# Condition maps of both layers as whole fp32 products on four quarters of the matrix array's columns

## The chip, the cores and the metric

The kernel runs on one core of one Trainium2 chip. The metric is the device time of one execution in microseconds (us), taken as the median of several runs; lower is better.

## The reference, cut to what matters

The reference is two layers of a hybrid trunk (windowed attention beside a state-space scan, then multi-head latent attention) on 1024 latent tokens and 128 context tokens of width 1024. Each layer begins with a norm that is shifted and scaled, and ends with a residual that is gated, and these three vectors come from a linear map of a condition vector. Latent and context tokens have one condition each:

```python
def modulation(cond, w_ada, b_ada):          # w_ada (1024, 3072) per layer, b_ada (3072,)
    m = jax.nn.silu(cond) @ w_ada + b_ada
    shift, scale, gate = jnp.split(m[:, None, :], 3, axis=-1)
    return shift, scale, gate

h = rms_norm(x, norm_w[layer]) * (1.0 + scale) + shift      # at the start of each layer
x = x + gate * out                                          # at its end
```

So each layer has a map of 2 rows by 1024 by 3072. It is small in arithmetic (two rows), but its weights are 12 MB per layer.

## The kernel before

**The condition maps.** `condition()` makes silu of both condition vectors with the contraction dimension on the partitions: `cond32[128, 8, 2]` in fp32, and `condT[128, 8, 4]`, which holds the rounded part and the remainder of both in float32r. `modulation(sp, l, j, parts)` then makes 256 of the 3072 columns of layer `l`, so there are 12 calls per layer and 24 in all. Columns j = 0..3 are the shift, 4..7 the scale, 8..11 the gate. Each call loads a bias row of 1 KB (L348) and four weight blocks of 128 x 2 x 256 (256 KB each, L301 in `raw_block`), and it has two forms:

- `parts` true (19 calls): `slab` splits each block into a rounded part (cast on ACT, L249) and a remainder (subtraction on DVE, L250). PE multiplies each of 8 contraction blocks with both parts: 16 float32r products with 4 stationary and 256 moving columns (L355, L356). The rows of `acc` are then latent and context of the rounded and of the remainder part of the condition.
- `parts` false (5 calls, all in the first stage): 8 fp32 products with 2 stationary columns, straight from the loaded block (L361). The trace has two records for each fp32 product, called passes here.

ACT copies `acc` to `rows` (L362), whose last row is the bias. A last product with the constant `sel` adds the rows of each condition and the bias: for shift and scale two fp32 products that also turn the columns to the partitions (L368), for the gate one (L376). DVE writes `shift` or `scl` (L371, L373); for the gate, ACT copies to `gs` (L378) and a DMA stores it in `gate_d`.

**Where the calls stand.** Eight calls (shift and scale of layer 0) are in the first stage, among the transposes of the normalised input (`hidden0`, L439) that need their results. The other sixteen are in the list `later`: one call of `some_modulation` makes the next one. Twelve are made in `convs` (the convolutions of layer 0, beside `attention0`), four in `gates1` (the gate projection of layer 1).

**What sets the order.** The code is built with a scheduler that places each engine's instructions by its own timing; only marked instructions stay in program order. All DMAs of loads and stores are issued by the SP engine, in its order, and a DMA whose destination is still in use holds up those behind it. Loaded weight blocks go through the ring `wr` of 8 buffers in fp32 (3 when the ring is reopened after the first stage), which the condition maps share with all split weights. `acc` and `pt` come from a PSUM ring of two, tag `tr`. `rows` has 2 buffers, `gs` one.

Of the kernel before, what the change touches and what calls it, by code (L numbers as in the profile page):

```python
# [15 lines left out]
ALU = mybir.AluOpType  # L16
# [38 lines left out]
def shape_constants():  # L55
    i = np.arange(128)
    ident = np.eye(128, dtype=np.float32)
    upper = (i[:, None] <= i[None, :]).astype(np.float32)
    lower = (i[:, None] >= i[None, :]).astype(np.float32)
    after = (i[:, None] > i[None, :]).astype(np.float32)  # L60
    before = (i[:, None] < i[None, :]).astype(np.float32)
    tri = np.stack([upper, lower, after, before, np.ones((128, 128), np.float32)], axis=1)
    c0, s0 = rope_tables(64)
    c1, s1 = rope_tables(32)
    rope0 = np.stack([c0, s0], axis=1)
    rope1 = np.stack([c1, s1], axis=1)
    rope1t = np.ascontiguousarray(np.stack([np.tile(c1.T, (4, 1)), np.tile(s1.T, (4, 1))], axis=1))
    sel = np.zeros((5, 2), np.float32)
    sel[[0, 2, 4], 0] = 1.0
    sel[[1, 3, 4], 1] = 1.0  # L70
    prev_ok = i[:, None] <= i[None, :]
    next_ok = i[:, None] >= i[None, :]
    mq = np.zeros((128, 640), np.float32)
    mq[:, 128:256] = np.where(prev_ok, 0.0, NEG)
    mq[:, 384:512] = np.where(next_ok, 0.0, NEG)
    mk = np.stack([np.where(prev_ok.T, 0.0, NEG), np.where(next_ok.T, 0.0, NEG)], axis=1).astype(np.float32)
    return {"k_ident": ident, "k_tri": tri, "k_rope0": rope0, "k_rope1": rope1, "k_rope1t": rope1t,
            "k_sel": sel, "k_mq": mq, "k_mk": mk}
# [142 lines left out]
def hybrid_trunk(ctx: ExitStack, tc: tile.TileContext, I, O, dbg=None, stage=99):  # L221
# [37 lines left out]


    ident = const("ident", [128, 128], I["k_ident"])
    sels = {n: const(f"sel{n}", [n + 1, 2], I["k_sel"][4 - n:5]) for n in (2, 4)}
    vecs = cp.tile([128, 96], F32, tag="vecs", name="vecs")
    shift = cp.tile([128, 2, KT, 2], F32, tag="shift", name="shift")
    scl = cp.tile([128, 2, KT, 2], F32, tag="scl", name="scl")
    cond32 = cp.tile([128, KT, 2], F32, tag="cond32", name="cond32")
    condT = cp.tile([128, KT, 4], F32R, tag="condT", name="condT")
    dts = cp.tile([128, NT, 32], F32, tag="dts", name="dts")
    normw = vecs[:, 0:16].rearrange("p (l k) -> p l k", l=2)

# [46 lines left out]
    def condition():  # L317
        with Space(mem) as p:
# [5 lines left out]
            dve.scalar_tensor_tensor(th, th, 1.0, cin, ALU.add, ALU.mult)  # L324
            pt = psum("tr", "pt")
            pe.transpose(pt[:, 0:16], th, ident[0:16, 0:16])
            full = cond32
            dve.tensor_scalar(full, pt[:, 0:16].rearrange("p (j k) -> p k j", j=2), 0.5, None, ALU.mult)
            split(condT[:, :, 0:2], condT[:, :, 2:4], full)
# [10 lines left out]
            dve.tensor_copy(vecs, pt[:, 0:96])  # L340
            dve.tensor_scalar(vecs[:, 16:76], vecs[:, 16:76], 0.5, None, ALU.mult)

    def modulation(sp, l, j, parts):

        c0 = j * 256
        n = 4 if parts else 2
        rows = cp.tile([5, 256], F32, tag="rows", name="rows", bufs=2)[0:n + 1]
        dma.dma_start(rows[n:n + 1], I["ada_b"][l:l + 1, c0:c0 + 256])  # L348
        acc = psum("tr", "acc")
        v = I["ada_w"][l].rearrange("(k p) n -> p k n", p=128)  # L350
        if parts:
            for k in range(KT):
                if k % 2 == 0:
                    wh, wl = slab(I["ada_w"][l], c0, rows=(k, k + 2), sp=sp, bufs=2)
                pe.matmul(acc[0:4, 0:256], condT[:, k], wh[:, k % 2], start=(k == 0), stop=False)  # L355
                pe.matmul(acc[0:4, 0:256], condT[:, k], wl[:, k % 2], start=False, stop=(k == KT - 1))  # L356
        else:
            for k in range(KT):
                if k % 2 == 0:
                    raw = raw_block([128, 2, 256], v[:, k:k + 2, c0:c0 + 256])  # L360
                pe.matmul(acc[0:2, 0:256], cond32[:, k], raw[:, k % 2], start=(k == 0), stop=(k == KT - 1))  # L361
        act.copy(rows[0:n], acc[0:n, 0:256])  # L362
        sel = sels[n]
        cg, ks = j // 4, slice((j % 4) * 2, (j % 4) * 2 + 2)
        if cg < 2:
            pt = psum("tr", "pt")
            for k in range(2):
                pe.matmul(pt[:, 2 * k:2 * k + 2], rows[:, k * 128:(k + 1) * 128], sel, start=True, stop=True)  # L368
            pv = pt[:, 0:4].rearrange("p (k j) -> p k j", j=2)
            if cg == 0:  # L370
                dve.tensor_copy(shift[:, l, ks], pv)  # L371
            else:
                dve.scalar_tensor_tensor(scl[:, l, ks], pv, 1.0, normw[:, l, ks].unsqueeze(2).broadcast_to([128, 2, 2]), ALU.add, ALU.mult)  # L373
        else:
            pt = psum("tr", "pt")
            pe.matmul(pt[0:2, 0:256], sel, rows, start=True, stop=True)  # L376
            gs = cp.tile([2, 256], F32, tag="gs", name="gs", bufs=1)
# [5 lines left out]
    def some_modulation(sp, n=1):  # L383
        for _ in range(n):
            if later:
                modulation(sp, *later.pop(0), True)

    def rstd_of(p, ssq, n, width):

# [52 lines left out]
            modulate(0, cond, k, hT[c][0][:, k, a:b], hT[c][1][:, k, a:b], pt[:, a:b], tmp[:, 0:b - a])  # L442
    for t in range(3):
        normalised(t)
    p1.reserve("wh", 512, 5, "R")
    p1.reserve("wl", 512, 5, "R")
    for j in range(4):
        modulation(p1, 0, j, False)
        modulation(p1, 0, 4 + j, j > 0)
        if j == 0:  # L450
            for t in range(3, 6):
                normalised(t)
        for c in range(2):
            for k in (2 * j, 2 * j + 1):
                hidden0(c, k)
# [391 lines left out]
    def convs(p):  # L847
# [18 lines left out]
        for n, sb in enumerate(order):  # L866
            for b in range(2):
# [19 lines left out]
                if fb < 9:  # L887
# [9 lines left out]
                some_modulation(p, 2 if b and n < 2 else 1)  # L897
                yield
        yield from beside
    p4, p = Space(mem), Space(mem)  # L900
# [3 lines left out]
    with Space(mem, right=True) as pa:  # L904
        cv = convs(p)
        at = attention0(pa)
        p.reserve("wh", 512, 2, "R")
        p.reserve("wl", 512, 2, "R")
# [318 lines left out]
    def gates1(p):  # L1227
# [8 lines left out]
        for n, (i, c) in enumerate(units):  # L1236
            if n % NCH == 0:
                weights(n // NCH + 2)
            dma.dma_start(g1_d[i, :, c * CH:(c + 1) * CH], silu_of(p, fm_proj(ws[i], 0, h1T, c)))
            if n < 8 and n % 2:  # L1240
                some_modulation(p)
            if n == 8:
                p.drop("wh", "wl")
            if i == 7:
                h1p.drop(f"h10{c}", f"h11{c}")
            yield
# [449 lines left out]
```

## Time and profile before

| | before |
|---|---|
| median of 3 runs | 1850.03 us |
| lowest and highest | 1843.2 and 1850.26 us |
| profiled execution, its own time | 1849.66 us |
| its span, first to last instruction | 1847.8 us |
| PE matmul busy | 1713.8 us (93% of the span) |
| PE weight load busy | 1315.1 us (71%) |
| DVE, ACT, POOL busy | 1045.4, 817.2, 744.2 us |
| mean granted TensorE clock | 0.958 |

PE is the matrix engine (PEld its weight loads), DVE, ACT and POOL the vector, scalar and general engines, SP the engine that issues the DMAs. A row of the profile names the line of the kernel, the engine, what is written and read, and the shapes: `128*4 128x256` is a product with 128 contraction rows and 4 stationary columns, 256 moving columns. Matmuls are pipelined, so the pace of a row of products is the distance from start to start, and not the duration of one.

### The profile page before, as it was taken

How to read it: one execution, taken by the hardware profiler on the slowest of the kernel's cores; microseconds unless marked ns; L12 is line 12 of the kernel's file. 1: busy time of each engine (PE TensorE's matmuls, PEld its weight loads, DVE VectorE, ACT ScalarE, POOL GpSimd, SP SyncE). 2: the span in 40 equal slices, each digit the busy share in tenths (PEclk: the TensorE clock that was granted, in tenths of full speed). 3: DMA queues.
4: the chain of work that ended last, by engine and by line, in shares of the span. 5: the costliest groups of instructions: out<-in, count | busy, mean ns of one | idle time of the engine just before them, and what ended most of it. 6: DMA issues, size and time to landing. Idle time of an engine off the chain costs nothing.

```text
span 1847.8 us, 27078 instructions
## 1 busy us (share of the span) xinstructions
PE 1713.8 (93%) x9031; PEld 1315.1 (71%) x9031; DVE 1045.4 (57%) x1989; ACT 817.2 (44%) x1873; POOL 744.2 (40%) x741
## 2 busy tenths in 40 slices
PE   6899999999998878998899999999999998998898
PEld 3799999877775766666688898655665665654486
DVE  4665545655546467777665434655665664564243
ACT  4532323665655354444444322444545544545321
POOL 3510000133343345665623010466666665565432
PEclk9999999999999888999999999899999998999899
DMA  7423423434435697565463532020120121104342
GB/s 260 125 81 93 121 62 111 131 101 132 115 105 146 195 284 240 166 208 159 167 180 85 165 110 79 11 61 23 52 71 23 45 75 28 37 29 122 109 154 91
DMA packets 210655, 210.26 MB, mean 114 GB/s; under 512 B 36162, under 2 KB 175504, under 8 KB 210516
## 3 DMA queue, kind: packets, MB, share of 16 engines
q1 hardware_dynamic: 210372, 208.40, 37.8%
q8 instruction: 72, 1.18, 0.3%
q14 instruction: 67, 0.55, 0.1%
q0 software_dynamic: 144, 0.13, 0.0%
HBM read 151.94 MB, written 51.72 MB: 110 GB/s over the span
## 4 chain that ended last, share of the span: by engine, by line
PE 65%; DMA 11%; DVE 8%; POOL 4%; ACT 3%; issue 3%; SPq 2%; POOLq 0%; DVEq 0%; ACTq 0%
PE acc L256 12%; PE acc L258 12%; PE acc L257 12%; PE acco L1469 6%; PE sc L1448 3%; PE pp L1427 3%; PE sc L1450 3%; PE sc L1449 3%; DMA arenaG<-cum_d 2%; DVE arenaR L250 2%; DMA arenaF<-rd_d 2%; DMA rd_d<-arenaF 2%; PE st L808 1%; DVE arenaF L209 1%; POOL arenaG L1003 1%
## 5 line engine op out<-in xcount | busy, mean ns | idle before, releaser
L256 PE MATMUL acc<-arenaR 128*128 128x384 f32 (+4 forms) x1248 | 426.7, 343 | 20.0 <-ACT arenaR L249 8.0
L1484 POOL TENSOR_TENSOR arenaG<-arenaG 128x512 f32<-128x512 f32 x256 | 332.6, 1318 | 233.8 <-ACT arenaG L1455 201.1
L257 PE MATMUL acc<-arenaR 128*128 128x384 f32 (+3 forms) x1176 | 398.2, 339 | 0.1
L258 PE MATMUL acc<-arenaR 128*128 128x384 f32 (+4 forms) x1152 | 385.9, 336 | 0.2
L256 PEld LDWEIGHTS acc<-arenaR 128*128 128x128 f32 x1248 | 240.0, 193 | 61.7 <-issue 16.0
L1455 ACT ACTIVATE arenaG<-sc 128x512 f32<-128x512 f32 (+1 forms) x304 | 174.7, 580 | 224.2 <-PE sc L1450 206.7
L209 DVE TENSOR_REDUCE arenaF<-pp 128x1 f32<-128x384 f32 (+1 forms) x400 | 198.8, 539 | 102.2 <-PE pp L1427 100.2
L257 PEld LDWEIGHTS acc<-arenaR 128*128 128x128 f32 x1176 | 226.4, 193 | 15.7 <-issue 3.6
L258 PEld LDWEIGHTS acc<-arenaR 128*128 128x128 f32 x1152 | 221.6, 192 | 16.5 <-DVE arenaR L250 2.3
L250 DVE TENSOR_TENSOR arenaR<-arenaF,arenaR 128x512 fp32r<-128x512 f32 (+2 forms) x144 | 133.2, 938 | 73.3 <-ACT arenaR L249 68.5
L249 ACT CAST arenaR<-arenaF 128x512 fp32r<-128x512 f32 (+3 forms) x160 | 101.0, 649 | 138.9 <-issue 22.6
L1469 PE MATMUL acco<-arenaG 128*64 128x512 f32 (+1 forms) x608 | 152.0, 612 | 0.0
L1005 ACT ACTIVATE arenaG<-arenaG,arenaF 128x128 f32<-128x128 f32 x288 | 88.4, 389 | 113.0 <-POOL arenaG L1003 112.7
L1427 PE MATMUL pp<-arenaR 96*128 96x384 f32 (+1 forms) x300 | 97.6, 387 | 12.8 <-DVE arenaF L209 12.5
L749 POOL TENSOR_TENSOR arenaG<-arenaF,arenaG 128x512 fp32r<-128x512 f32 x28 | 47.8, 1708 | 150.8 <-PE acco L753 87.0
L1448 PE MATMUL sc<-arenaR 96*128 96x512 f32 (+1 forms) x228 | 94.9, 416 | 5.6 <-ACT arenaG L1455 5.4
L1427 PEld LDWEIGHTS pp<-arenaR 96*128 96x128 f32 x300 | 58.6, 203 | 57.3 <-DVE arenaF L209 28.4
L1450 PE MATMUL sc<-arenaR 97*128 97x512 f32 (+1 forms) x228 | 90.6, 400 | 1.0 <-DMA arenaR<-arenaF 1.0
L258 PE MATMUL acc<-arenaR,arenaS 128*128 128x512 f32 (+1 forms) x240 | 90.6, 382 | 0.0
L1449 PE MATMUL sc<-arenaR 96*128 96x512 f32 (+1 forms) x228 | 89.9, 394 | 0.0
L1469 PEld LDWEIGHTS acco<-arenaG 128*64 128x64 f32 x608 | 37.3, 141 | 71.4 <-issue 68.3
L1003 POOL TENSOR_SCALAR_AFFINE_SELECT arenaG<-arenaG 128x512 f32<-128x512 f32 x72 | 60.2, 859 | 63.3 <-DMA arenaG<-cum_d 56.4
(328 smaller groups left out, 3331.9 us busy)
## 6 DMA issues: line engine op xcount, KB each, us to landing
arenaF<-in_ada_w_dram SPq DMA_DIRECT2D x96, 256.0 KB
arenaG<-cum_d SPq DMA_DIRECT2D x36, 512.0 KB
arenaF<-in_ab_w_in_dram SPq DMA_DIRECT2D x51, 256.0 KB
z_d<-arenaF SPq DMA_DIRECT2D x36, 128.0 KB
xs_d<-arenaF SPq DMA_DIRECT2D x8, 576.0 KB
arenaF<-xs_d SPq DMA_DIRECT2D x9, 512.0 KB
arenaF<-z_d SPq DMA_DIRECT2D x9, 512.0 KB
x_d<-arenaG SPq DMA_DIRECT2D x9, 512.0 KB
```

Of the source, the lines that this page charges most:

```text
L209: f()
L250: lo_eng.tensor_tensor(lo, src, hi.bitcast(F32), ALU.subtract)
L256: pe.matmul(out, ah, bh, start=first, stop=False)
L257: pe.matmul(out, ah, bl, start=False, stop=False)
L258: pe.matmul(out, al, bh, start=False, stop=last)
L1427: pe.matmul(pp[:, 0:w], AQ[s][0:96, t * 128:(t + 1) * 128], AK[s][0:96, k0:k0 + w], start=True, stop=True)
L1448: pe.matmul(sc[:, 0:n], AK[s][0:96, ks], BQ[s][:, qs], start=True, stop=False)
L1449: pe.matmul(sc[:, 0:n], BK[s][:, ks], AQ[s][0:96, qs], start=False, stop=False)
L1450: pe.matmul(sc[:, 0:n], AK[s][:, ks], AQ[s][:, qs], start=False, stop=True)
L1455: act.activation(pf, sc[:, 0:n], AF.Exp, scale=SCALE_M)
L1469: put = lambda: pe.matmul(acc[0][a * 64:(a + 1) * 64], V[:, a], pfs[a], start=(i < 2 and k < 2), stop=(last and k >= len(todo) - 2))
L1484: pool.tensor_tensor(totals[a], first[a] if i == 1 else totals[a], pfs[a], ALU.add)
```

## The change

All 24 calls now take one form, in fp32 from the loaded block. `condT`, the splits of the condition weights and the parameter `parts` are gone, as are the split buffers that were reserved for them in three places.

- `cond32` is widened to 32 columns per contraction block, all but two of them zero (a memset on POOL).
- A call makes 16 fp32 products with 32 stationary and 128 moving columns. The quarter i of the output partitions, and so of the array's columns, takes contraction block k + i // 2 and the half i % 2 of the 256 columns. After four rounds over the four quarters, the sum of quarters 0 and 2 is the first half of the result, that of 1 and 3 the second.
- ACT copies `acc`, now 128 x 128, to `rows`. For each half, a product with the constant `sel[:, half]` adds the two quarters, and a second product with `ones2` adds the bias: four fp32 products per call in place of two (shift, scale) or one (gate).
- Bias and gate output share one buffer, `edge`, of which there is one: partition 0 for the bias, partitions 32 and 33 for `gs`.

```diff
-    def modulation(sp, l, j, parts):
+    def modulation(l, j):
...
-        rows = cp.tile([5, 256], F32, tag="rows", name="rows", bufs=2)[0:n + 1]
-        dma.dma_start(rows[n:n + 1], I["ada_b"][l:l + 1, c0:c0 + 256])
+        edge = cp.tile([34, 256], F32, tag="edge", name="edge", bufs=1)
+        bias, gs = edge[0:1], edge[32:34]
+        dma.dma_start(bias, I["ada_b"][l:l + 1, c0:c0 + 256])
         acc = psum("tr", "acc")
         v = I["ada_w"][l].rearrange("(k p) n -> p k n", p=128)
-        if parts:
-            for k in range(KT):
-                if k % 2 == 0:
-                    wh, wl = slab(I["ada_w"][l], c0, rows=(k, k + 2), sp=sp, bufs=2)
-                pe.matmul(acc[0:4, 0:256], condT[:, k], wh[:, k % 2], start=(k == 0), stop=False)
-                pe.matmul(acc[0:4, 0:256], condT[:, k], wl[:, k % 2], start=False, stop=(k == KT - 1))
-        else:
-            for k in range(KT):
-                if k % 2 == 0:
-                    raw = raw_block([128, 2, 256], v[:, k:k + 2, c0:c0 + 256])
-                pe.matmul(acc[0:2, 0:256], cond32[:, k], raw[:, k % 2], start=(k == 0), stop=(k == KT - 1))
-        act.copy(rows[0:n], acc[0:n, 0:256])
-        sel = sels[n]
+        for k in range(0, KT, 2):
+            raw = raw_block([128, 2, 256], v[:, k:k + 2, c0:c0 + 256])
+            for i in range(4):
+                pe.matmul(acc[i * 32:(i + 1) * 32, 0:128], cond32[:, k + i // 2], raw[:, i // 2, i % 2 * 128:(i % 2 + 1) * 128], start=(k == 0), stop=(k == KT - 2))
+        rows = cp.tile([128, 128], F32, tag="rows", name="rows", bufs=2)
+        act.copy(rows, acc[:, 0:128])
         cg, ks = j // 4, slice((j % 4) * 2, (j % 4) * 2 + 2)
+        pt = psum("tr", "pt")
+        for h in range(2):
+            part = bias[:, h * 128:(h + 1) * 128]
+            if cg < 2:
+                pe.matmul(pt[:, 2 * h:2 * h + 2], rows, sel[:, h], start=True, stop=False)
+                pe.matmul(pt[:, 2 * h:2 * h + 2], part, ones2, start=False, stop=True)
+            else:
+                pe.matmul(pt[0:2, h * 128:(h + 1) * 128], sel[:, h], rows, start=True, stop=False)
+                pe.matmul(pt[0:2, h * 128:(h + 1) * 128], ones2, part, start=False, stop=True)
...
-    p1.reserve("wh", 512, 5, "R")
-    p1.reserve("wl", 512, 5, "R")
     for j in range(4):
-        modulation(p1, 0, j, False)
-        modulation(p1, 0, 4 + j, j > 0)
+        modulation(0, j)
+        modulation(0, 4 + j)
```

The scheduler places the new instructions anew. Lines from 237 on stand a few numbers lower or higher in the changed kernel: there L355 are the products, L357 the copy, L363 and L364 the sums of a shift or scale call (`rows` and bias), L366 and L367 those of a gate call, L349 the bias load, L304 a weight block's load.

In the program of each engine, the shape at the end of a row is the output's. First a stretch of PE's program in `convs`, where a shift or scale call of layer 1 is made, in the kernel before (L740 to L753 are the products of `attention0`, L256 to L258 a convolution's projection):

```order
L256 MATMUL acc<-arenaR 128x384
L257 MATMUL acc<-arenaR 128x384
L258 MATMUL acc<-arenaR 128x384
L355 MATMUL acc<-arenaR,condT 4x256
L256 MATMUL acc<-arenaR 128x384
L257 MATMUL acc<-arenaR 128x384
L258 MATMUL acc<-arenaR 128x384
L753 MATMUL acco<-arenaG 65x512
L751 MATMUL acco<-arenaG 65x512
L752 MATMUL acco<-arenaG 64x512
L356 MATMUL acc<-arenaR,condT 4x256
L355 MATMUL acc<-arenaR,condT 4x256
```

The same call's counterpart in the changed kernel:

```order
L355 MATMUL acc<-arenaF,cond_78 32x128 x12
L748 MATMUL acco<-arenaG 65x512
L746 MATMUL acco<-arenaR,arenaG 65x512
L747 MATMUL acco<-arenaR,arenaG 64x512
L735 MATMUL sc<-arenaR,arenaG 128x512
L738 MATMUL sc<-arenaR,arenaG 128x512
L748 MATMUL acco<-arenaG 65x512
L746 MATMUL acco<-arenaG 65x512
L747 MATMUL acco<-arenaG 64x512
L355 MATMUL acc<-arenaF,cond_78 32x128 x4
```

Where sixteen products stood in groups of 8, 1 and 7, there are now one group of 12 and, some products of others later, one of 4; the most common pattern in `convs` and `gates1` is this 12 and 4.

Second, SP's program at the end of the first stage, from the bias of the second last call there to the weights of the first projection (L592, L593), in the kernel before:

```order
L348 DMA rows<-in_ada_b_dram 1x256
L592 DMA arenaF<-in_ab_w_in_dram 128x256
L593 DMA arenaF<-in_ab_w_in_dram 128x32
L592 DMA arenaF<-in_ab_w_in_dram 128x256
L593 DMA arenaF<-in_ab_w_in_dram 128x32
L348 DMA rows<-in_ada_b_dram 1x256
L592 DMA arenaF<-in_ab_w_in_dram 128x256
L593 DMA arenaF<-in_ab_w_in_dram 128x32
L592 DMA arenaF<-in_ab_w_in_dram 128x256
L544 DMA arenaF<-in_k_rope_dram 128x9x128
```

And in the changed kernel, where L587 and L588 load those projection weights and L426 loads the last three input tiles:

```order
L349 DMA edge<-in_ada_b_dram 1x256
L541 DMA arenaF<-in_ab_dt_bias_dram 128x32
L543 DMA arenaF<-in_ab_sink_dram 128x8
L579 DMA arenaF<-in_cache_a_k_dram 128x128
L580 DMA arenaF<-in_cache_a_v_dram 128x128
L587 DMA arenaF<-in_ab_w_in_dram 128x256
L588 DMA arenaF<-in_ab_w_in_dram 128x32
L426 DMA arenaS<-in_x_sample_dram 128x1024 x2
L426 DMA arenaS<-in_x_prompt_dram 128x1024
L349 DMA edge<-in_ada_b_dram 1x256
L587 DMA arenaF<-in_ab_w_in_dram 128x256
L588 DMA arenaF<-in_ab_w_in_dram 128x32
```

The bias of the last call of the first stage, with only one `edge` to load it into, has moved behind three input loads of 512 KB, and one block of the projection's weights is loaded ahead of it where there were two.

More of the change, by code (lines that the diff above doesn't have):

```diff
@@ L67, in shape_constants @@
     rope1t = np.ascontiguousarray(np.stack([np.tile(c1.T, (4, 1)), np.tile(s1.T, (4, 1))], axis=1))
-    sel = np.zeros((5, 2), np.float32)
-    sel[[0, 2, 4], 0] = 1.0
-    sel[[1, 3, 4], 1] = 1.0
+    sel = np.zeros((128, 2, 2), np.float32)
+    for half in range(2):
+        for cond in range(2):
+            sel[[32 * half + cond, 64 + 32 * half + cond], half, cond] = 1.0
     prev_ok = i[:, None] <= i[None, :]
@@ L261, in hybrid_trunk @@
     ident = const("ident", [128, 128], I["k_ident"])
-    sels = {n: const(f"sel{n}", [n + 1, 2], I["k_sel"][4 - n:5]) for n in (2, 4)}
+    sel = const("sel", [128, 2, 2], I["k_sel"])
+    ones2 = cp.tile([1, 2], F32, tag="ones2", name="ones2")
+    pool.memset(ones2, 1.0)
     vecs = cp.tile([128, 96], F32, tag="vecs", name="vecs")
@@ L265, in hybrid_trunk @@
     scl = cp.tile([128, 2, KT, 2], F32, tag="scl", name="scl")
-    cond32 = cp.tile([128, KT, 2], F32, tag="cond32", name="cond32")
-    condT = cp.tile([128, KT, 4], F32R, tag="condT", name="condT")
+    cond32 = cp.tile([128, KT, 32], F32, tag="cond32", name="cond32")
+    pool.memset(cond32, 0.0)
     dts = cp.tile([128, NT, 32], F32, tag="dts", name="dts")
@@ L326, in condition @@
             pe.transpose(pt[:, 0:16], th, ident[0:16, 0:16])
-            full = cond32
-            dve.tensor_scalar(full, pt[:, 0:16].rearrange("p (j k) -> p k j", j=2), 0.5, None, ALU.mult)
-            split(condT[:, :, 0:2], condT[:, :, 2:4], full)
+            dve.tensor_scalar(cond32[:, :, 0:2], pt[:, 0:16].rearrange("p (j k) -> p k j", j=2), 0.5, None, ALU.mult)
             vrow = p.tile([96, 128], F32, name="vrow")
@@ L341, in condition @@
             dve.tensor_scalar(vecs[:, 16:76], vecs[:, 16:76], 0.5, None, ALU.mult)
-    def modulation(sp, l, j, parts):
+    def modulation(l, j):
         c0 = j * 256
-        n = 4 if parts else 2
-        rows = cp.tile([5, 256], F32, tag="rows", name="rows", bufs=2)[0:n + 1]
-        dma.dma_start(rows[n:n + 1], I["ada_b"][l:l + 1, c0:c0 + 256])
+        edge = cp.tile([34, 256], F32, tag="edge", name="edge", bufs=1)
+        bias, gs = edge[0:1], edge[32:34]
+        dma.dma_start(bias, I["ada_b"][l:l + 1, c0:c0 + 256])
@@ L365, in modulation @@
         if cg < 2:
-            pt = psum("tr", "pt")
-            for k in range(2):
-                pe.matmul(pt[:, 2 * k:2 * k + 2], rows[:, k * 128:(k + 1) * 128], sel, start=True, stop=True)
             pv = pt[:, 0:4].rearrange("p (k j) -> p k j", j=2)
@@ L374, in modulation @@
         else:
-            pt = psum("tr", "pt")
-            pe.matmul(pt[0:2, 0:256], sel, rows, start=True, stop=True)
-            gs = cp.tile([2, 256], F32, tag="gs", name="gs", bufs=1)
             act.copy(gs, pt[0:2, 0:256])
@@ L381, in hybrid_trunk, with some_modulation @@
     later = [(0, 8 + j) for j in range(4)] + [(1, j) for j in range(12)]
-    def some_modulation(sp, n=1):
+    def some_modulation(n=1):
         for _ in range(n):
             if later:
-                modulation(sp, *later.pop(0), True)
+                modulation(*later.pop(0))
     def rstd_of(p, ssq, n, width):
@@ L896, in convs @@
                         beside = chunk_states(p, fb, xt, Bt)
-                some_modulation(p, 2 if b and n < 2 else 1)
+                some_modulation(2 if b and n < 2 else 1)
                 yield
@@ L906, in hybrid_trunk @@
         at = attention0(pa)
-        p.reserve("wh", 512, 2, "R")
-        p.reserve("wl", 512, 2, "R")
         next(cv)
@@ L1240, in gates1 @@
             if n < 8 and n % 2:
-                some_modulation(p)
-            if n == 8:
-                p.drop("wh", "wl")
+                some_modulation()
             if i == 7:
```

## The prediction

> **What bounds the kernel now.** The page comes first: busy shares, and the chain that ended last.
>
> ```profile
> span 1847.8 us, 27078 instructions
> PE 1713.8 (93%) x9031; PEld 1315.1 (71%) x9031; DVE 1045.4 (57%) x1989; ACT 817.2 (44%) x1873; POOL 744.2 (40%) x741
> PE 65%; DMA 11%; DVE 8%; POOL 4%; ACT 3%; issue 3%; SPq 2%; POOLq 0%; DVEq 0%; ACTq 0%
> ```
>
> PE is busy for 93% and carries 65% of the chain, so an edit counts first by the PE time that it takes away, and then by the waits of PE. That is an average, and the 24 calls stand in three stages: eight in the first 72 us, twelve in 328 to 640, four in 1016 to 1070. The busy time of those stretches (columns: length, then PE, PEld, DVE, ACT, POOL with instruction counts, granted clock, DMA share, GB/s), and one of 4 us from the first stage:
>
> ```profile
> 0.00:72.00 72.00, 50.45 (x280) 29.55 (x281) 40.66 (x79) 40.92 (x85) 30.63 (x51) 0.97 0.73 235
> 328.00:640.00 312.00, 286.27 (x1560) 226.79 (x1559) 171.97 (x279) 178.59 (x362) 102.43 (x104) 0.96 0.47 134
> 1016.00:1070.00 54.00, 52.92 (x319) 46.96 (x318) 22.78 (x45) 21.75 (x48) 0.00 (x0) 1.00 0.56 165
> 16.00:20.00 4.00, 3.55 (x18) 1.49 (x17) 0.16 (x1) 1.15 (x2) 0.00 (x0) 1.00 1.01 376
> ```
>
> The three differ. From 1016 to 1070 PE has 1.1 us without work, so only PE's own time counts there. From 328 to 640 it lacks 26 us, and DVE and ACT are a little over half busy: here waits can go. In the first stage PE is idle for 21.6 us of 72 and the DMA share is 0.73, reaching 1.01 around 16 to 20: transfers set a good part of the pace, and PE time saved is not all time won. The waits of PE, the first three rows from 328 to 640 and the last from 1016 to 1070 (total, times, longest):
>
> ```profile
> PE pt L368 <- ACT rows L362: 3.4, 1, 3.4
> PE acc L355 <- ACT arenaR L249: 2.8, 2, 2.1
> PE acc L356 <- DVE arenaR L250: 2.2, 2, 1.6
> ...
> PE acc L355 <- ACT arenaR L249: 0.6, 1, 0.6
> ```
>
> The condition products wait there for their splits for 2.8 + 2.2 = 5.0 us, and later for 0.6.
>
> **The change part by part.** *The products of the 19 split calls.* A group of eight, and the first product after it, in PE's timeline:
>
> ```profile
> 328.10 0.36 PE L355 MATMUL acc<-arenaR,condT 128*4 128x256 f32 x1
> ...
> 329.09 0.34 PE L256 MATMUL acc<-arenaR 128*128 128x384 f32 x1
> ```
>
> Eight take 329.09 - 328.10 = 0.99 us, sixteen 1.98. No row has fp32 products on four quarters of the columns; the nearest has two halves (128*64 fp32, both filled), against products that write 64 columns one after the other:
>
> ```profile
> 1306.79 0.44 PE L1469 MATMUL acco<-arenaG 128*64 128x128 f32 x4
> 1307.16 0.45 PE L1427 MATMUL pp<-arenaR 96*128 96x384 f32 x1
> ...
> 395.62 0.65 PE L808 MATMUL st<-arenaS,arenaF 128*64 128x128 f32 x4
> 396.20 0.50 PE L740 MATMUL sc<-arenaG 128*128 128x512 f32 x1
> ```
>
> Four passes of 128 columns take 0.58 us in turn and 0.37 in halves, so two passes cost 0.21, 0.105 each. With quarters a round of eight passes is, if the four run as the two do, 0.37 for the first round and 0.21 for each further one. For the two further quarters I add one weight load to each group:
>
> ```profile
> L361 PEld LDWEIGHTS acc<-arenaF,cond 128*2 128x2 f32 x80 | 6.7, 91 | 12.1 <-issue 5.6
> ```
>
> Twelve products (three rounds) then take 0.37 + 2 x 0.21 + 0.09 = 0.88, four take 0.46: 1.34 per call. The gain is 0.64 per call, 12.2 over 19 calls. The ends: 0.79 + 0.37 = 1.16 without the load, and 32 passes x 0.105 = 3.36 with the lead of two groups (2 x 0.16, the 0.37 less two passes), 3.7, if nothing runs side by side. I take 1.34, by the row of the halves, since it is fp32 on column parts.
>
> *The products of the 5 fp32 calls.*
>
> ```profile
> 35.48 3.62 PE L361 MATMUL acc<-arenaF,cond 128*2 128x256 f32 x16
> 39.03 0.33 PE L439 MATMUL pt<-ident,arenaS 128*128 128x128 f32 x1
> ```
>
> 39.03 - 35.48 = 3.55 becomes 1.34: 2.2 less, 11.0 for five.
>
> *The sums behind them,* which grow from two fp32 products to four (shift, scale) and from one of 256 columns to four of 128 (gate):
>
> ```profile
> 430.15 0.60 PE L368 MATMUL pt<-sel,rows 5*128 5x2 f32 x4
> 430.69 0.33 PE L781 MATMUL pt<-ident,arenaF 128*128 128x128 f32 x1
> ...
> 339.90 0.59 PE L376 MATMUL pt<-rows,sel 5*2 5x256 f32 x2
> 340.42 0.28 PE L355 MATMUL acc<-arenaR,condT 128*4 128x256 f32 x1
> ```
>
> Two products take 0.54, though they move two columns each; four take 1.08. Sixteen such calls cost 16 x 0.54 = 8.6. A gate call goes from 0.52 to eight passes x 0.105 and the same lead of 0.16, 1.0: eight calls cost 3.8. All of it is on PE. The ends are 0.105 x 4 = 0.42 and 0.54 more per call.
>
> By stage, PE's own time then changes by 8 x 0.54 - 5 x 2.2 - 3 x 0.64 = -8.6 in the first, by 8 x 0.54 + 4 x 0.48 - 12 x 0.64 = -1.5 from 328 to 640, by 4 x 0.48 - 4 x 0.64 = -0.6 in the last.
>
> The Trainium skill, "TensorE: Matmul & The Clock Gate", section "Measured speedup vs the span model", speaks against full overlap: three column tiles gave 2.38 times, 0.79 a tile. By that, four would give about 3.2, so that the six slots of twelve products and two of four grow by a quarter (8 x 0.105 x 0.25 = 0.2 per call, an estimate), and the result would be near 1843. No run here shows four column parts.
>
> *Casts and subtractions.* Nineteen calls lose four casts and four subtractions each, 76 of each:
>
> ```profile
> L249 ACT CAST arenaR<-arenaF 128x512 fp32r<-128x512 f32 x129 | 77.9, 622 | 68.0 <-DMA arenaF<-in_ab_w_in_dram 21.3 <-DMA arenaF<-in_ada_w_dram 15.5 <-DMA arenaF<-in_mla_w_out_dram 10.8
> L250 DVE TENSOR_TENSOR arenaR<-arenaF,arenaR 128x512 fp32r<-128x512 f32 x121 | 102.4, 859 | 50.9 <-ACT arenaR L249 46.3 <-PE acc L257 3.3 <-PE acc L258 0.8
> ```
>
> That is 76 x 0.622 = 47 us of ACT and 76 x 0.859 = 65 us of DVE, beside PE's work. Worth on the path: the 5.0 and the 0.6 go whole, as no split is left to wait for. Next late is the transfer of the block itself; at a DMA share of 0.47 I cost it at nothing. From 328 to 640, 48 casts and 48 subtractions leave (30 and 41 us), and the attention's softmax and the convolutions on both engines come earlier; PE waits for them too, and I take 2 us, between 0 and the 3.4 of the L368 row. ACT's copy of `acc`, now 128 x 128 for 4 x 256, has fewer elements per partition and I cost it at nothing. The wider `cond32` needs a memset that ends before PE's first product, at nothing.
>
> *The order of DMAs.* A raw block's buffer now comes free with PE's products and not with DVE's subtraction:
>
> ```profile
> SPq L301 <- DVE arenaR L250: 46.7, 28, 4.6
> ```
>
> SP waits there now (320 to 720); it will wait for PE, which runs the group of 12 when the last of three blocks is there. I cost this at nothing: the wait moves, and PE's waits in that stage were mostly others. The single `edge` is new. The bias of a call waits on SP until the last sum of the call before has read it, and for a gate until the stored `gs` has landed; behind it on SP stand the weight blocks of this call and all other loads. A small load takes about this:
>
> ```profile
> 4.02 0.25 SPq L337 DMA_DIRECT2D arenaF<-in_mla_q_norm_w_dram  x1
> ...
> 5.44 0.39 PE L339 MATMUL pt<-ident,arenaF 96*128 96x96 f32 x1 [0.70 <-DMA arenaF<-in_mla_q_norm_w_dram]
> ```
>
> 1.4 us from issue to use. In `convs` calls stand far apart and the bias is asked for one call early, so it is hidden; SP's holds after the eight gate calls, about 1.4 each (11 us of SP), I cost at 2. No call stands from 72 to 328 or behind 1070, and those stretches I leave as they are. In the first stage the calls are dense: the last bias stands behind three 512 KB inputs (at 376 GB/s 4.2 us), and PE cannot pass its bias product. I take 2 us, between 0 and 4.2 + 1.4 = 5.6.
>
> **The sum.** First stage: of 8.6 I take 6, since transfers share that stage, less 2 for the bias: -4 (ends -8.6 and +5.6). 328 to 640: -1.5 - 5.0 - 2 = -8.5 (ends -12 and 0). 1016 to 1070: -0.6 - 0.6 = -1.2. SP's holds: +2. Together -11.7. The profiled execution took 1849.66, its span and 1.9 around it, 0.4 under the median of 1850.03; so 1850 - 11.7 gives 1838. Terms near their ends give 1829 to 1845.
>
> **The rivals.**
> - *The gain is hidden.* The first stage keeps its end because transfers set it (for it: the share of 1.01; against it: the PE rows of the fp32 calls fill 3.55 of 4 us), and of the 7 us of waits half come back elsewhere: -1.5 - 3.5 - 1.2 + 2 = -4, 1846; with the bias's 2 us, 1848.
> - *Slower: the one `edge`.* If the bias arrives late at every call, PE stands at the bias product in all three stages, up to 1.4 us each, 34 over 24 calls. Against it: only in the first stage does the order put the bias close before its use. It decides from 0.9 per call (21 us), where 1838 becomes 1859; with 1.0, 1862.
> - *The change does not do what it says: quarters do not run side by side.* In turn, a call's products take 3.7: 19 x 1.7 + 5 x 0.15 = 33 for products in place of -23, 1838 + 56 = 1894, some 1885 with the first stage's part hidden. If only two run at a time (16 x 0.105 + 0.3 = 2.0) it is 1852. Against it: the halves.
> - *Quarters overlap less than halves.* If each slot of side by side passes takes 0.13 us where I take 0.105, the eight slots of a call take 0.2 more, 24 calls 4.8: 1843. For it: with four parts in work, four weight loads and four streams of 128 rows share what two share in the row of the halves; against it: there the second two passes add exactly one slot. The page named above, with its 2.38 for three, is for it.
> - *The clock rises.* From 328 to 640 it was 0.96, and a product of the condition map was at times slowed from 0.28 to 0.41 us:
>
> ```profile
> 328.41 0.28 PE L355 MATMUL acc<-arenaR,condT 128*4 128x256 f32 x1
> ...
> 417.70 0.41 PE L355 MATMUL acc<-arenaR,condT 128*4 128x256 f32 x1
> ```
>
>  Without the waits for splits, 0.04 x 312 = 12 us could come back, say three quarters: 1829. The Trainium skill, "TensorE: Matmul & The Clock Gate", section "HAM oscillation — how this bites in real kernels", has the clock halve after an idle window of about 3.4 us. Of the condition products' waits in that stage none is that long (the longest is 2.1 us), and by that rule this rival gains nothing.
>
> **How the numbers follow.** Forecast 0.48, hidden gain 0.18, `edge` 0.10, less overlap 0.10, quarters in turn or in pairs 0.07, clock 0.07. The range 1825 to 1860 leaves out most of the `edge` case, the serial quarters and the forecast's tails, under 0.2; the forecast's own is 1829 to 1845. A measurement of this kernel can tell about 0.5%, 9 us, from no change: faster is below 1841, slower above 1859. Faster has three quarters of the forecast, the clock and a third of the less overlap: 0.46. The same has the rest of both and the hidden gain: 0.37 (with the quarters in pairs). Slower is `edge`, the quarters in turn and a few hundredths for the upper ends of the bias's wait: 0.17.
>
> **What would show it.** Right: a group of twelve L355 at about 0.9 us and of four at about 0.5; L363 and L364 together 1.1; casts (L249) and subtractions (L250) of 128x512 down by 76 each; the end of the first stage some 4 us earlier, the stretch to 640 some 8 shorter, the rest alike. Wrong: rounds much longer than 0.25; waits of PE at L364 or L367 for the bias of more than 5 us in all; a first stage that ends at 72 or later; or a change after 1070, where nothing that the change touches is left.

## The result and the profile after

Over 20 executions each, the changed kernel has a median of 1864.74 us (1852.06 to 1876.21) and the kernel before 1853.81 us. The ratio is 1.0058, with a 95% interval of 1.0037 to 1.0079: slower by 0.6%, about 11 us, where 1838 was forecast; the time lies above the range.

The first profile of the changed kernel happens to be its slowest execution (1876.21). Experiment e1 profiled the same program again at 1859.78, nearer to the median, and the lines below are of that one where nothing else is said. The head of its page:

```profile
span 1857.7 us, 27868 instructions
PE 1726.5 (93%) x9527; PEld 1337.5 (72%) x9527; DVE 980.3 (53%) x1912; ACT 778.1 (42%) x1796; POOL 723.6 (39%) x743
```

DVE and ACT lost 65 and 39 us of work (65 and 47 forecast), but PE, from which 10.7 us were to go, has 12.7 more. To see where, here are the same windows as before (the granted clock is the third number from the right), and with them one that the prediction did not look at, the scan of layer 0 and its output projection:

```profile
0.00:72.00 72.00, 53.11 (x446) 42.87 (x447) 30.87 (x69) 34.18 (x74) 31.72 (x56) 0.86 0.74 239
328.00:640.00 312.00, 290.32 (x1840) 233.42 (x1839) 140.07 (x236) 158.87 (x322) 93.07 (x108) 0.96 0.48 137
640.00:1016.00 376.00, 328.54 (x1489) 259.78 (x1488) 237.22 (x347) 157.65 (x430) 175.37 (x201) 0.88 0.60 181
```

The kernel before, in the last of these windows:

```profile
640.00:1016.00 376.00, 334.83 (x1610) 269.85 (x1609) 258.59 (x377) 167.74 (x462) 195.42 (x221) 0.92 0.60 185
```

In the same 376 us PE gets through 1489 instructions in place of 1610, at a clock of 0.88 in place of 0.92. There is no call of `modulation` in that stage. Marks read from PE's timeline tell it by stages:

| mark | before | changed (e1) | difference |
|---|---|---|---|
| last transpose of `hidden0`, in the first stage (L439, L436) | 84.42 | 80.88 | -3.54 |
| first transpose of the queries, behind that stage (L643, L638) | 127.54 | 127.94 | +0.40 |
| last transpose of `convs` (L892, L887) | 616.34 | 608.06 | -8.28 |
| first product of the scan with the carried state (L992, L985) | 678.10 | 678.02 | -0.08 |
| fifth chunk of the scan, first product (L1011, L1004) | 795.54 | 792.97 | -2.57 |
| ninth and last chunk, last product (same lines) | 937.70 | 952.70 | +15.00 |
| last transpose of the latents, behind the scan (L1173, L1166) | 1015.76 | 1033.20 | +17.44 |
| last product of the program | 1839.53 | 1849.31 | +9.78 |

`convs` ends 8 us early, near the forecast; all of it is given back on the way into the scan, where the first product L992 (changed: L985) comes at 678 in both, and 2.6 us are ahead again at the fifth chunk; the loop over the chunks then loses 17.6, and 20.0 by the end of the latents. (From 1137 to 1727, in the attention of layer 1, this execution was 10 us quicker than the profile of before; the other profile of the same program was not. From the last transpose of the latents to the end the sixteen profiles take 816 to 830 us, whatever the kernel, so that is scatter.) The loop alone, five chunks, before and changed:

```profile
795.60:937.80 142.20, 126.34 (x620) 96.86 (x619) 102.44 (x126) 61.63 (x180) 84.71 (x87) 0.95 0.53 170
```

```profile
793.00:952.80 159.80, 146.14 (x645) 111.07 (x644) 99.10 (x130) 65.65 (x190) 83.20 (x89) 0.87 0.51 155
```

A fifth of the stretch grew from 28.4 to 32.0 us. Up to this mark PE does not wait longer: its idle time is 142.2 - 126.3 = 15.9 us before and 13.7 now. What grew is busy time, and the clock says why: by an estimate from its column, 0.05 x 142.2 = 7 us went to the throttle before and 0.13 x 159.8 = 21 now, 14 of the 17.6.

The mark does not cut off the same work, however: the changed order has 645 PE instructions ahead of it and the old one 620, and behind it PE waits for 8 us, which it does not do before. Up to the last transpose of the latents the work is the same, 994 or 995 instructions. The wait, and that longer stretch before and changed:

```profile
961.24 1.94 PE L1015 MATMUL pt<-ident,arenaF 128*128 128x128 f32 x8 [8.27 <-DVE arenaF L1010]
```

```profile
795.60:1015.80 220.20, 199.46 (x995) 163.44 (x994) 150.96 (x233) 96.20 (x274) 111.47 (x141) 0.95 0.51 156
793.00:1033.20 240.20, 214.12 (x994) 173.83 (x994) 146.85 (x241) 99.18 (x282) 107.59 (x140) 0.89 0.49 145
```

So with equal work the order costs 20 us: 26.1 us idle in place of 20.7, which is 5 us of waits, and 15 us more of busy time, at a lower clock.

One chunk in stretches of 4 us, before and changed:

```profile
826.00:830.00 4.00, 2.79 (x17) 2.30 (x18) 2.85 (x4) 1.94 (x5) 3.17 (x5) 0.80 0.70 195
830.00:834.00 4.00, 2.83 (x8) 0.82 (x4) 4.00 (x3) 0.55 (x3) 4.00 (x4) 0.77 0.61 218
834.00:838.00 4.00, 3.82 (x25) 3.38 (x26) 4.00 (x8) 2.07 (x8) 0.62 (x1) 1.00 0.59 182
```

```profile
826.00:830.00 4.00, 2.37 (x11) 1.26 (x10) 2.02 (x3) 2.94 (x10) 3.83 (x5) 1.00 1.03 284
830.00:834.00 4.00, 3.30 (x10) 2.07 (x10) 3.82 (x6) 1.17 (x2) 1.35 (x2) 0.53 0.92 255
834.00:838.00 4.00, 4.00 (x13) 3.02 (x13) 0.01 (x1) 1.34 (x5) 1.88 (x3) 0.50 0.29 93
838.00:842.00 4.00, 4.00 (x19) 3.45 (x19) 3.49 (x6) 1.10 (x4) 0.00 (x0) 0.69 0.36 131
```

And PE's timeline there, the waits in brackets, before and changed:

```profile
827.96 1.58 PE L1022 MATMUL pt<-ident,arenaF 128*128 128x128 f32 x8 [1.22 <-DVE arenaF L1017]
...
831.97 0.39 PE L257 MATMUL acc<-arenaR,arenaS 128*128 128x512 f32 x1
...
834.18 0.99 PE L1011 MATMUL yacc<-arenaF,arenaG 128*128 128x64 f32 x7 [1.35 <-DVE arenaG L1008]
```

```profile
830.70 1.97 PE L1015 MATMUL pt<-ident,arenaF 128*128 128x128 f32 x8 [2.24 <-DVE arenaF L1010]
...
835.62 0.63 PE L257 MATMUL acc<-arenaR,arenaS 128*128 128x512 f32 x1
...
840.57 0.40 PE L257 MATMUL acc<-arenaR,arenaS 128*128 128x512 f32 x1
```

In this chunk, before, two pauses of 1.2 and 1.35 us stand apart, and the clock is low for about 4 us behind the first. Changed, one pause of 2.24 us is followed by some 10 us at half the clock, in which a product that takes 0.39 us takes 0.63.

The length of the pause does not decide this. The kernel before has a longer one, 2.94 us, in the next chunk, with under 4 us of low clock behind it; and in e5, a run below with the same order of the loop, a pause of 2.94 us has none:

```profile
864.27 1.10 PE L1011 MATMUL yacc<-arenaF,arenaG 128*128 128x64 f32 x8 [2.94 <-DVE arenaG L1008]
...
866.00:870.00 4.00, 4.00 (x15) 3.07 (x14) 3.20 (x6) 0.16 (x1) 0.53 (x1) 0.58 0.58 201
```

```profile
827.30 1.10 PE L1030 MATMUL yacc<-arenaF,arenaG 128*128 128x64 f32 x8 [2.94 <-DVE arenaG L1027]
...
820.00:840.00 20.00, 16.23 (x87) 12.80 (x86) 16.89 (x20) 6.02 (x19) 11.37 (x10) 1.00 0.53 163
```

What differs is the sum over the loop: at half the clock for 0.05 x 142.2 / 0.5 = 14 us before, and for 0.13 x 159.8 / 0.5 = 41 us changed. What in the new order brings on the long stretches stays open.

### The profile page after: what moved, and what is told of

Its sections match the earlier page's. It is cut to its first block, busy times and chain, and to the rows that moved or that the text cites. A ratio compares the mean times of both kernels' runs of the same rounds, so it can differ in the third digit from the quotient of the medians.

```text
span 1874.3 us, 27868 instructions
## 1 busy us (share of the span) xinstructions
PE 1738.4 (93%) x9527; PEld 1344.0 (72%) x9527; DVE 982.9 (52%) x1912; ACT 778.6 (42%) x1796; POOL 721.7 (39%) x743
## 4 chain that ended last, share of the span: by engine, by line
PE 36%; DMA 6%; DVE 4%; ACT 2%; issue 2%; SPq 1%; POOL 1%; DVEq 0%; POOLq 0%; ACTq 0%
PE acc L257 6%; PE acc L258 6%; PE acco L1460 6%; PE acc L259 5%; PE sc L1439 3%; PE pp L1418 3%; PE sc L1441 3%; PE sc L1440 3%; DMA arenaF<-rd_d 2%; DMA rd_d<-arenaF 2%; PE den L1491 1%; DVE arenaF L210 1%; DVE arenaF L1263 1%; DVE arenaR L251 1%; DMA arenaF<-in_mla_w_in_dram 1%
## 5 line engine op out<-in xcount | busy, mean ns | idle before, releaser
L257 PE MATMUL acc<-arenaR 128*128 128x384 f32 (+4 forms) x1248 | 428.2, 344 | 20.8 <-ACT arenaR L250 8.8
L258 PE MATMUL acc<-arenaR 128*128 128x384 f32 (+4 forms) x1248 | 421.0, 337 | 1.4 <-DVE arenaR L251 1.4
L259 PE MATMUL acc<-arenaR 128*128 128x384 f32 (+4 forms) x1152 | 387.3, 337 | 0.3 <-DVE arenaR L254 0.2
L257 PEld LDWEIGHTS acc<-arenaR 128*128 128x128 f32 x1248 | 240.9, 193 | 63.5 <-issue 19.2
L258 PEld LDWEIGHTS acc<-arenaR 128*128 128x128 f32 x1248 | 241.2, 193 | 17.3 <-issue 2.7
L259 PEld LDWEIGHTS acc<-arenaR 128*128 128x128 f32 x1152 | 221.9, 193 | 18.4 <-issue 3.7
L251 DVE TENSOR_TENSOR arenaR<-arenaF,arenaR 128x512 fp32r<-128x512 f32 (+3 forms) x84 | 79.3, 950 | 54.9 <-ACT arenaR L250 53.2
L250 ACT CAST arenaR<-arenaF 128x512 fp32r<-128x512 f32 (+3 forms) x84 | 55.8, 670 | 96.9 <-issue 22.4
L744 POOL TENSOR_TENSOR arenaG<-arenaF,arenaG 128x512 fp32r<-128x512 f32 x26 | 36.2, 1392 | 144.4 <-PE acco L748 126.1
L996 POOL TENSOR_SCALAR_AFFINE_SELECT arenaG<-arenaG 128x512 f32<-128x512 f32 x72 | 52.6, 753 | 83.7 <-DMA arenaG<-cum_d 77.2
```

What stands on the lines that cost most here:

```text
L251: lo_eng.tensor_tensor(lo, src, hi.bitcast(F32), ALU.subtract)
L257: pe.matmul(out, ah, bh, start=first, stop=False)
L258: pe.matmul(out, ah, bl, start=False, stop=False)
L259: pe.matmul(out, al, bh, start=False, stop=last)
```

## The experiments

Theory O, later L: the scheduler gave the scan's loop, which the change does not touch, another order, and that order is the loss. Rivals: the stage is slow because of how it is entered (S), or the calls themselves are dear (D).

In the kernels called *held*, the instructions of one stretch are chained per engine in the order that another kernel has there. The chain sets the order alone and adds no wait (shortened; `traced` is the stretch in the order of the code, `HELD` the other kernel's order):

```python
traced = nc.cur_bb.bb.instructions[start:end]
for engine, order in HELD.items():
    mine = [i for i in traced if engine_of(i) == engine]
    for a, b in zip(order, order[1:]):
        tc.add_manual_dep(mine[b], mine[a].name, NoSync, reason="held")
```

### e1, e2, e3 and e4: the whole stage held

e1 is the changed kernel once more. e2 is the changed kernel with the stage from `gates0` to the last output projection in the order of before, e3 the reverse. e4 is e2 with two places for bias and gate output, taken in turn at partitions 0 and 64:

```diff
-        edge = cp.tile([34, 256], F32, tag="edge", name="edge", bufs=1)
-        bias, gs = edge[0:1], edge[32:34]
+        at = next(turn)
+        bias, gs, one = edges[at:at + 1], edges[at + 32:at + 34], ones2[at:at + 1]
```

> The changed kernel once more, for a second profile. In the first one the stages up to the end of the convolutions ended within 3 us of before, the scan and output projection of layer 0 (about 650 to 995 us) took some 24 us longer than before, and the rest was alike. Every theory: ratio to before 1.004 to 1.008. If the loss is of the program's order (theory O), it stands in the same stage in this profile, at +8 to +25 us; if it was a bad execution only (rival), it is spread or gone there.

> The changed kernel, with every engine's instructions of the scan and output stage of layer 0 chained in the order that the scheduler gave them in the kernel before (order only, no waits added); that stage holds none of the changed instructions. Theory O (the loss is the order that the scheduler newly made there): the loss goes, 1845 to 1853 us, ratio 0.995 to 0.999. Rival S (the stage is slow because of how and when it is entered, with whatever order): 1860 to 1868, as the changed kernel. Rival D (the loss is in the calls themselves, in their sums and in waits for the weights): also 1860 to 1868.

> The kernel before, with the same stage chained in the order that the scheduler gave it in the changed kernel. Theory O: slower by what the changed kernel loses there, 1862 to 1872, ratio 1.005 to 1.010. Rivals S and D: as the kernel before, ratio 0.998 to 1.002.

> As e2, with two places for bias and gate output in place of one, so that the next call's bias load does not wait for the last sum of the call before. If the single buffer costs, this is 2 to 6 us faster than e2, with SP's waits on it gone and the first stage ending 1 to 3 us earlier; if not, as e2 within 2 us (the order of the other stages is made anew too, which may move it by some us either way).

Measured: e1 1860.65 us, ratio 1.0056 (1.0035 to 1.0077), the loss in the same loop. e3 1872.33, 1.0104 (1.0082 to 1.0127): the changed kernel's order makes the kernel before slow, as theory O has it. But e2 came to 1864.85, 1.0065 (1.0041 to 1.0089), no better than the changed kernel. Its profile shows part of why: the loop's five chunks went from 159.8 to about 144.5 us, but the fifth chunk was reached 7.5 us later than in e1, so the loop ended only 8 us earlier. That the old order does not fit the way into the loop, which comes out of `convs` at another moment, is an argument and not shown; and the profiles of e2 and of e5 below are 14 us apart where their medians are 20 apart. e4, 1866.44 and 1.0084 (1.0063 to 1.0105), is no faster than e2: the single `edge` costs nothing that can be seen.

### e5 and e6: only the loop held

> The changed kernel with only the loop over the chunks of the scan (one chunk's scan beside the output projection of the one before, about 700 to 990 us) chained in the order it had in the kernel before; the entry to that stage keeps the changed kernel's order. In the profiles so far the changed kernel's order takes 32 us per chunk there, that of before 28.4. Theory L (that order is what the change costs): the loop is 14 to 18 us shorter than in the changed kernel, the whole 1846 to 1852 us, ratio 0.996 to 1.000. Rival S (the order only shifts where PE stands, and the time comes back as pauses or a lower clock elsewhere in the stage): the loop is shorter, but the whole stays at 1858 to 1866.

> The kernel before with the same loop chained in the order of the changed kernel. Theory L: 1866 to 1872 us, ratio 1.007 to 1.010, all of it in the loop. Rival S: 1852 to 1860.

e5 has a median of 1844.72 us, ratio 0.9964 (0.9943 to 0.9985); e6 1869.95, 1.0108 (1.0085 to 1.0131). Both are what theory L said, and rival S falls for the loop. The loop in e5:

```profile
789.70:932.10 142.40, 126.27 (x619) 97.47 (x619) 102.98 (x126) 61.36 (x180) 84.92 (x87) 0.95 0.54 171
```

And in e6:

```profile
800.50:959.50 159.00, 145.62 (x644) 110.18 (x644) 99.01 (x130) 65.78 (x190) 83.59 (x90) 0.88 0.52 156
```

Over all profiles without filling, those with the order of before take 142 to 148 us for the five chunks, at a clock of 0.91 to 0.95, and those with the other 159 to 163, at 0.86 to 0.88. With the loop's order equal the change is worth -0.36%, about -7 us (3 to 11); the order costs 1.0058 - 0.9964 = 0.94%, 17 us, near the loop's 17.6. e5 is also faster than both kernels.

### e7 and e8: the first stage in the old forms, and two places again

> The first stage's eight calls in the old forms (five plain fp32, three split), the sixteen later ones in the new form. The scheduler gives the chunk loop nearly the order of before here by itself. Theory L with G (the first stage's saved PE time is paid back as pauses and halved clock): the clock that is lost in the first 110 us goes from 12 back to some 3.4 us and that stage ends within 1 us of before; the loop takes about 28.4 us per chunk; the whole 1843 to 1851, ratio 0.994 to 0.999. If the new form itself costs (rival D), 1858 to 1864.

> As e5, with two places for bias and gate output. In the profile of e4 the first stage was some 6 us shorter than in e2, which had one. If that is the single buffer's price, 3 to 7 us less than e5: 1841 to 1848; if it was chance, within 2 us of e5.

e7: 1848.85 us, 0.9991 (0.9965 to 1.0016). Its loop took 145.2 us, by the scheduler's own choice, and the new form in the sixteen later calls costs nothing that can be seen (rival D falls); nor does this run show a gain, as its interval includes 1. The clock of the first 72 us is back at 0.95:

```profile
0.00:72.00 72.00, 51.85 (x280) 30.74 (x280) 40.30 (x77) 39.98 (x81) 31.01 (x52) 0.95 0.73 234
```

In the changed kernel it was 0.86: 0.14 x 72 = 10 us to the throttle, against 0.03 x 72 = 2 before. These 8 us are near the 8.6 us of PE time that were to go in that stage; that the saved time was spent on the lower clock is likely and not shown. Whether the new form of the first eight calls is worth anything can't be told from e5 and e7, whose intervals overlap. e8: 1847.48, 0.9973 (0.9955 to 0.9990), again no gain by a second `edge`.

### e9, e10 and e11: the pause filled

Theory C says that the order costs by the clock. Twelve products that nobody reads, chained just ahead of the transposes, keep PE at work through the pause; the waits stay as they are (the edit, shortened):

```diff
             pt = psum("tr", "pt")
+            for _ in range(12 if q == 0 and 0 < c < NLT else 0):
+                pe.matmul(pt[:, 0:128], ident, ident, start=True, stop=True)
             for j in range(4):
                 pe.transpose(pt[:, j * 128:(j + 1) * 128], y[:, ...], ident)
```

> The changed kernel with the chunk loop chained in its own order, and in each of seven chunks 12 fp32 products of 128 columns that nobody reads, on PE just ahead of the transposes of the normalised scan output (2.6 us of PE work where PE now stands still for 1.3 to 2.8 us). They take no wait away; they only keep PE at work. In the profiles, that pause is followed by some 10 us at half the granted clock in most chunks of the changed kernel (low for 40 us of the loop's 160), and for 4 us in the kernel before. Theory C (the order costs by the clock: its pauses are followed by longer stretches at half clock): low stretches in the loop fall from 40 to under 20 us, the loop from 160 to 146 to 152, the whole 1850 to 1858. Rival W (the order costs by its waits): the loop stays at 160 or grows by the filling (up to 7 x 1 us), the whole 1862 to 1872.

> As e5 (the changed kernel, chunk loop in the order of before), with the same filling products. By theory C the low stretches there, 16 us in e5, go partly, 3 to 6 us less, 1839 to 1843; but the pause there is only 1.25 us, so the filling also delays the transposes by about 1.3 us a chunk, up to 9 us in all. By rival W it is slower than e5 by 3 to 9 us.

> The kernel before with its own order of the chunk loop and the same filling products, to see whether the filling by itself moves a kernel without the change: as e10 against e5, ratio to before 0.996 to 1.004 by theory C, 1.002 to 1.005 by rival W.

The loop in e9, and the same place in a chunk (L1042 are the filling products, L1045 the transposes, which now begin without a wait):

```profile
796.00:944.60 148.60, 145.60 (x765) 115.06 (x765) 100.00 (x129) 65.38 (x190) 83.61 (x91) 0.98 0.56 170
```

```profile
830.76 1.12 PE L1013 MATMUL off<-arenaG,arenaF 64*128 64x512 f32 x2
831.81 2.94 PE L1042 MATMUL pt<-ident 128*128 128x128 f32 x24
834.71 1.09 PE L1045 MATMUL pt<-ident,arenaF 128*128 128x128 f32 x8
```

PE has more to do and the loop is 11 us shorter: 148.6 us in place of 159.8, at 0.98 in place of 0.87. That is theory C; by rival W the loop could not have become shorter. Up to the last transpose of the latents 9 of the order's 20 us are gone (231.3 us in place of 240.2), while behind the last chunk a wait of 6.4 us stays, so a part of the cost is left that the waits explain and the clock does not. The whole time follows by less, 1858.41 us, ratio 1.0031 (1.0006 to 1.0056), just above theory C's range, and its interval overlaps that of the changed kernel. In the order of before the filling raises the clock as well, to 0.99 in e10 and 0.98 in e11, but the loop stays at 141 and 143 us. It gains nothing that can be told, and the 3 to 6 us expected of e10 did not come: e10 1847.94, 0.9977 (0.9951 to 1.0003), and e11 1852.38, 0.9993 (0.9972 to 1.0015).

### e12: whole weights without the quarters

All 24 calls take the old fp32 form (L361, 8 products of 256 columns), and the loop is held in the order of before:

```diff
-        modulation(p1, 0, 4 + j, j > 0)
+        modulation(p1, 0, 4 + j, False)
...
-                modulation(sp, *later.pop(0), True)
+                modulation(sp, *later.pop(0), False)
```

> The weights whole in fp32 in all 24 calls, as in the change, but without the quarters: 8 products of 2 stationary and 256 moving columns per call, bias and sums as before; chunk loop in the order of before, so it stands beside e5. By the rows a call's products take 3.55 us in place of 1.15, its sums 0.6 less: 1.8 more per call, 28 over the sixteen later ones, of the first eight's 14 up to all hidden by transfers. Theory Q (the quarters carry the direct gain): 1872 to 1887, ratio 1.011 to 1.019. Rival H (leaving out casts and subtractions carries it, PE has room): 1845 to 1855.

1867.69 us, 1.0090 (1.0070 to 1.0110): 23 us above e5. Theory Q has the sign right, and the time lies below its range; leaving out casts and subtractions does not carry the gain, the quarters do.

### e13 and e14: whose order

> As e5, but in the chunk loop only PE's order is that of before; the other engines' order is the scheduler's. If PE's order makes the pause ahead of the transposes long (theory P), the loop takes 142 to 146 us and the whole 1843 to 1850, ratio 0.995 to 1.000. If it is the order of the transfers and of the vector engines (rival V), the loop takes 155 to 160 and the whole 1858 to 1866.

> As e5, but in the chunk loop the order of all engines but PE is that of before; PE's is the scheduler's. Theory P: the loop stays near 155 to 160 us, 1856 to 1866. Rival V: 142 to 146, 1843 to 1850.

e13 came to 1848.65 us, 0.9989 (0.9964 to 1.0014), e14 to 1844.32, 0.9963 (0.9941 to 0.9986); their loops took 142.8 and 143.2 us. Either half of the order brings back the short loop, but the two runs do not separate the halves: in both traces the loop's instructions stand on every engine almost as they do before, so with one side held the scheduler places the other side alike. Which move in the changed kernel's order costs the time stays open.

## Why the prediction was wrong

**The step that failed** is the list of what moves: no call stands from 72 to 328 or behind 1070, "and those stretches I leave as they are". The stage from 640 to 1016 was not priced at all, and the last paragraph took "the rest alike". It holds no changed instruction, but the scheduler placed its loop anew, and that is the 17 us between e5 and the result. e3 and e6 show it from the other side: the kernel before, given that order, becomes 1% slower. The order of the whole program could be read beforehand: its differences did not end with the last call in `convs`, and each stretch with another order was a cost with unknown sign that had no place in the sum or among the rivals.

**The direct part** was right in sign and high in size: -11.7 forecast, about -7 measured with the loop's order equal (e5, whose interval reaches from -3 to -11). Term by term, from the changed kernel's first profile, where twelve products and then four, and the sums of a shift and a gate call, read so:

```profile
332.42 0.86 PE L355 MATMUL acc<-arenaF,cond 128*32 128x128 f32 x24
333.21 0.44 PE L748 MATMUL acco<-arenaG 128*65 128x512 f32 x1
...
339.38 0.43 PE L355 MATMUL acc<-arenaF,cond 128*32 128x128 f32 x8
339.73 0.44 PE L257 MATMUL acc<-arenaR 128*128 128x384 f32 x1
...
423.56 0.28 PE L363 MATMUL pt<-sel,rows 128*128 128x2 f32 x2
...
424.70 0.54 PE L355 MATMUL acc<-arenaF,cond 128*32 128x128 f32 x12
...
346.27 0.38 PE L366 MATMUL pt<-rows,sel 128*2 128x128 f32 x2
...
347.50 0.30 PE L355 MATMUL acc<-arenaF,cond 128*32 128x128 f32 x1
```

- *Products*: 0.79 and 0.35 us, 1.14 per call against 1.34: the lower end, without the added weight load. A further round of eight passes costs (0.79 - 0.35) / 2 = 0.22, what two passes cost in halves, so from round to round the quarters run fully side by side. The two rivals on the quarters fall. (The case of two at a time adds up to 1838 + 24 x 0.66 = 1854, not to the 1852 of the prediction.) The Trainium skill, "TensorE: Matmul & The Clock Gate", section "Measured speedup vs the span model", has 2.38 for three column tiles. A lone round agrees with a loss of that kind: 0.35 us against 8 x 0.105 + 0.16 = 1.0 in turn (an estimate from the prediction's rows) is 2.9 for four. A further round does not: 0.22 against 0.84 is nearly all of four, and the extra 0.2 per call worked out from the 2.38 did not come.
- *Sums*: 424.70 - 423.56 = 1.14 (forecast 1.08) and 347.50 - 346.27 = 1.23 (forecast 1.0). Right but for a tenth or two.
- *Casts*: 129 of the 128x512 form became 53, 76 less, as forecast.
- *Waits from 328 to 640*: the 5.0 us for the splits went, as forecast, but the transfer behind them, costed at nothing, was not free. Its row in e1:

```profile
PE acc L355 <- DMA arenaF<-in_ada_w_dram: 10.9, 6, 3.6
```

 The waits of that attention product for POOL (L753, 7.0 before; L748, 0.5 now) went in turn, and from the queries to the end of `convs` e1 gained 8.7 us (from +0.4 to -8.3) beside the forecast 8.5: right in sum, but through other terms, and not in each profile. The first one gained 5.9 there, and e7, with the same calls, 1.6.
- *First stage*: -4 forecast. Its last transpose comes 3.5 us earlier in e1 and 1.6 in the first profile, but at the first transpose of the queries nothing is left of it (+0.4 and +2.4). That last transpose stands at 84 us before, so the prediction's stretch of 72 us did not hold the whole stage. The bias did not hold it up: PE's waits for `edge` come to 0.5 us in e1, and e4 and e8 show no gain. The clock fell from 0.97 to 0.86, and this column even says too little. The trace has no clock for its first 31 us, which then reads as 1.00, while a whole call runs there at the pace of half clock. Three calls of e1, and between them one of its stretches of 4 us:

```profile
27.74 1.93 PE L355 MATMUL acc<-arenaF,cond 128*32 128x128 f32 x32
28.00:32.00 4.00, 4.00 (x43) 3.15 (x36) 2.25 (x4) 1.70 (x4) 3.47 (x4) 1.00 0.77 241
...
36.21 1.08 PE L355 MATMUL acc<-arenaF,cond 128*32 128x128 f32 x32
...
48.69 1.94 PE L355 MATMUL acc<-arenaF,cond 128*32 128x128 f32 x32
```

 The last of them stands where the clock reads 0.50. In the kernel before, a whole call takes as long here as the one that the prediction shows at 35.48, so full pace is there before 20 us:

```profile
19.47 3.62 PE L361 MATMUL acc<-arenaF,cond 128*2 128x256 f32 x16
```

 The first clock in the trace, a full one, comes at 14 to 17 us in the six kernels with the old forms in this stage (before, e3, e6, e7, e11, e12), and at 28 to 52 us in the ten with the new one. What of this is time lost on the path is not shown.
- *The way into the scan* gave back the 8 us of `convs` up to its product L992, and 6 of them up to the fifth chunk. In e5 it gave back 3 of 9 (the fifth chunk comes 6.0 us early), and the program ends 6.3 us early. That term was missing too.

**The rivals.** The slower one, the single `edge`, was the wrong mechanism. The one on the clock had the right mechanism with the wrong sign, and in another stage: it was thought of as something to win back. It had a chance of 0.07, held down by the Trainium skill, "TensorE: Matmul & The Clock Gate", section "HAM oscillation — how this bites in real kernels", by which idle time over about 3.4 us halves the clock. The trace does not bear that length out as a limit: up to the last product of the two loops above no wait of PE is longer than 2.94 us, and the clock was at half for 14 and 41 us of them all the same.

## What to carry to other kernels

Where a scheduler orders the program, compare the order of every stage, and also of those that the edit does not touch; give each stage that differs a term with both signs, or hold its order and measure the edit alone. Look at a loop's granted clock beside its idle time: two orders of the same work differed by 20 us, of which the waits made up 5. Compare two orders between marks that hold the same instructions. Time taken from PE in a stage that something else paces is not won for certain; here such a stage ran at half pace for longer.

## What the runs showed of the hardware that was not expected

- Four fp32 products on quarters of the columns, 32 stationary and 128 moving columns each, cost 0.22 us a round; two passes alone cost 0.21.
- One pause of 2.24 us was followed by about 10 us at half the clock, another of 2.94 us (e5) by none. Twelve products that nobody reads, in each pause of this kind, raised the loop's clock from 0.87 to 0.98 and made it 11 us shorter (e9); in the other order the clock rose from 0.95 to 0.99 and the loop stayed within 2 us (e5, e10).
- The granted clock read 1.00 at the start of a trace while whole calls took 1.93 us, as at 0.50 later, and not 1.08 (e1). The paces of equal products tell it where the column can't.
